# Holding back five of six early loads until VectorE's first memset has ended

## The chip, the cores and the metric

The kernel runs on one core of a Trainium2 chip. The metric is device time in microseconds (us) of one execution, as the median of several runs. One more execution was recorded by the hardware profiler; all views of the profile below are of that one.

## The reference

Scores of an attention layer, without the softmax: for each of 8 x 8 pairs of batch and head, every one of 512 queries with every one of 512 keys.

```
q, k: (8, 8, 512, 64) float32
scale = 1 / sqrt(64)
out[b, h, i, j] = sum over d of q[b, h, i, d] * k[b, h, j, d] * scale     # (8, 8, 512, 512) float32
```

The inputs are 16.8 MB, the output is 67.1 MB.

## The kernel before

The batch is worked through in four units of two batches each (`UNITS = 4`). A unit has one tile of k and one of q, each 128 partitions x 16 KB, so there are eight loads of 2 MB; they are numbered here load 0 (k of unit 0), load 1 (q of unit 0), load 2 (k of unit 1) and so on to load 7. Each unit gives four chunks of output (`CHUNKS = 4`), and each of the 16 chunks is stored with one DMA of 4 MB. Three large buffers (`bigs`) serve both the loaded tiles and the finished chunks.

The way of the data: SyncE issues a load (`load`, L78). GpSimd waits for it to land, and casts it to bf16 in two halves, in an order that suits the next step (L122, into `xb`); after the second half it raises `ready`. TensorE transposes the casts through an identity matrix (L130), moving two bf16 values as one float32 word. ScalarE and VectorE copy the transposes to `kT` and `qz` (L184). `qz` holds each query block beside zeros, and the zeros are written once, at the start, by two memsets on VectorE (L189), each raising `zeroed` by one. Then TensorE multiplies (L145), eight pairs of matmuls for a chunk, and ScalarE (L209) and VectorE (L212) take turns in scaling the pairs into the chunk's buffer. When both have done four, SyncE issues the store (L96).

The order on each engine is the order in which the program lists its instructions; semaphores, written out by hand, hold the engines together. The only part inside the scheduler's frame is load 0: `tc.close()` at L84 ends the frame, and its barriers stand at L85 in the profile. So load 0 is issued ahead of the barriers, and all else follows them.

On SyncE everything goes through one queue, in this order: load 0; the barriers; loads 1 to 5, with no wait between them; load 6 after `ready` has reached 3, and load 7 after it has reached 4, since these two fill a buffer again that an earlier unit used; then the 16 stores, each behind its waits for ScalarE and VectorE; and at the end the waits for the last stores.

VectorE's list begins, behind the barriers, with the two memsets of `qz`, and then goes on to the copies of the first transposes. GpSimd's begins with the identity matrix and then waits for load 0. On ScalarE the third copy waits until `zeroed` is 2, as does VectorE's.

Of the kernel before, what the change touches and what calls it, by code (L numbers as in the profile page):

```python
# [5 lines left out]
def kernel(  # L6
# [5 lines left out]
    nc = tc.nc  # L12
# [25 lines left out]
    sem = {name: nc.alloc_semaphore(name) for name in names}  # L38
# [38 lines left out]
    def load(v, x):  # L77
        nc.sync.dma_start(out=xf(v)[:, x],  # L78
                          in_=(k_r, q_r)[x][v].rearrange("p (s c) -> p s c", s=2)
                          ).then_inc(load_sems[2 * v + x], 16)  # L80
# [4 lines left out]
    tc.compile()  # L85


    for n in range(1, 2 * (UNITS - 1)):
        load(n // 2, n % 2)
    for x in range(2):  # L90
# [154 lines left out]
```

## Time and profile before

| | us |
|---|---|
| median of 3 runs | 201.34 (201.3 to 201.4) |
| the profiled execution | 201.4 |
| its span, from the first to the last instruction | 200.1 |
| load 0, issue to landing | 7.84 |
| load 1, issue to landing | 11.3 |
| a store, issue to landing, median | 21.9 |
| a cast of half a load on GpSimd (16 of them) | 2.46 |
| a memset of `qz` on VectorE (2) | 3.47 |

Times in the views are counted from the start of the span. SPq is SyncE's queue: its rows are the instructions that issue DMAs, and their duration is the time that SyncE spends on issuing, not that of the transfer. The transfer shows as "issue to landing", or as "DMA" in the chain of waits. A "window" is a stretch of the span: the view gives the busy time of each engine in it, the granted clock of TensorE, the busy share of the 16 DMA engines and the rate in GB/s. DMA engines are not to be confused with the engines that compute; a load of 128 rows of 16 KB is 128 packets, eight for each DMA engine, and a packet is counted in the window in which it starts.

### The profile page before, as it was taken

The page shows a single profiled execution, that of the slowest core. Times are in us where ns is not written, and L with a number is a line of the kernel's source. Part 1 is how long each engine was busy: PE and PEld are TensorE (multiplying, and loading weights), DVE is VectorE, ACT ScalarE, POOL GpSimd, SP SyncE. Part 2 cuts the span into 40 slices and gives each one's busy share as a digit, 9 for nine tenths or more (in the row PEclk, how much of TensorE's full clock was granted, in tenths as well). Part 3 has the DMA queues.
Part 4 walks back from the last instruction along what each step waited for, and adds up shares of the span by engine and source line. Part 5 has one row for each costly group of instructions (what it writes and reads, how often), then busy time and mean ns, then how long its engine had stood idle before and what let it go on. Part 6 is the DMA issues. An engine that isn't in the chain of part 4 may idle for free.

```text
span 200.1 us, 1081 instructions
## 1 busy us (share of the span) xinstructions
PE 100.4 (50%) x377; PEld 47.6 (24%) x384; DVE 106.1 (53%) x98; ACT 84.7 (42%) x97; POOL 39.4 (20%) x22
## 2 busy tenths in 40 slices
PE   0027660376785966376547646872737373830000
PEld 0026530142431532143124313330202020200000
DVE  3825692076796679276917682767364544450000
ACT  2004670264694657265626653664444443430000
POOL 1299999996000000000000000000000000000000
PEclk9999997579797599889957995799696968585555
DMA  6999999999999999999999999999999999999996
GB/s 197 426 423 436 439 429 423 426 409 429 416 442 436 429 423 436 436 426 429 429 432 436 429 426 439 429 429 423 439 426 432 423 442 429 429 426 429 432 439 259
DMA packets 5509, 83.95 MB, mean 420 GB/s; under 512 B 384, under 2 KB 384, under 8 KB 384
## 3 DMA queue, kind: packets, MB, share of 16 engines
q1 hardware_dynamic: 5504, 83.89, 98.6%
q8 instruction: 3, 0.05, 0.1%
q14 instruction: 2, 0.02, 0.0%
HBM read 16.78 MB, written 67.11 MB: 419 GB/s over the span
## 4 chain that ended last, share of the span: by engine, by line
DMA 54%; DVE 12%; POOL 12%; PE 10%; issue 1%; SPq 0%
DMA out_dram<-big 42%; POOL xb L122 12%; DVE big L212 10%; DMA big<-in_q_dram 7%; PE ps L145 7%; DMA big<-in_k_dram 4%; PE tp L130 3%; DVE qz L184 2%; DVE kT L184 1%; SPq L95 0%; SPq L85 0%; SPq L82 0%
## 5 line engine op out<-in xcount | busy, mean ns | idle before, releaser
L145 PE MATMUL ps<-kT,qz 128*128 128x512 bf16 x249 | 80.0, 455 | 61.3 <-DMA out_dram<-big 31.5
L212 DVE TENSOR_SCALAR big<-ps 128x1024 f32<-128x1024 f32 x64 | 77.0, 1223 | 52.0 <-PE ps L145 50.0
L209 ACT ACTIVATE big<-ps 128x1024 f32<-128x1024 f32 x64 | 65.0, 1023 | 70.8 <-PE ps L145 67.8
L145 PEld LDWEIGHTS ps<-kT,qz 128*128 128x128 bf16 x256 | 25.3, 110 | 109.4 <-DMA out_dram<-big 34.9
L122 POOL CAST xb<-big 128x2048 bf16<-128x2048 f32 x16 | 38.7, 2463 | 6.4 <-DMA big<-in_k_dram 5.8
L130 PE MATMUL tp<-identity,xb 128*128 128x128 f32 x104 | 19.6, 352 | 13.8 <-POOL xb L122 13.8
L130 PEld LDWEIGHTS tp<-identity,xb 128*128 128x128 f32 x104 | 17.6, 188 | 17.6 <-issue 16.3
L184 DVE COPY kT<-tp 64x512 f32<-64x512 f32 x14 | 9.7, 694 | 9.2 <-PE tp L130 8.8
L184 ACT COPY kT<-tp 64x512 f32<-64x512 f32 x14 | 8.1, 577 | 14.4 <-PE tp L130 14.2
L184 DVE COPY qz<-tp 64x512 f32<-64x512 f32 x12 | 8.3, 694 | 4.4 <-PE tp L130 4.0
L189 DVE MEMSET qz<- 128x4096 uint32 x2 | 6.9, 3472 | 4.1 <-PEq L85 3.3
L184 ACT COPY qz<-tp 64x512 f32<-64x512 f32 x12 | 7.4, 620 | 2.1 <-PE tp L130 2.0
L130 PE MATMUL ps<-identity,xb 128*128 128x128 f32 x24 | 5.4, 414 | 1.2 <-POOL xb L122 1.2
L130 PEld LDWEIGHTS ps<-identity,xb 128*128 128x128 f32 x24 | 5.0, 227 | 1.6 <-POOL xb L122 1.6
L184 DVE COPY qz<-ps 64x512 f32<-64x512 f32 x4 | 2.8, 694 | 1.9 <-PE ps L130 1.7
L184 ACT COPY qz<-ps 64x512 f32<-64x512 f32 x4 | 2.5, 632 | 2.2 <-PE ps L130 2.2
L184 ACT ACT_TABLE_LOAD x1 | 1.3, 1283 | 2.3 <-PEq L85 2.3
L184 DVE COPY kT<-ps 64x512 f32<-64x512 f32 x2 | 1.4, 694 | 0.3 <-PE ps L130 0.3
L184 ACT COPY kT<-ps 64x512 f32<-64x512 f32 x2 | 1.2, 578 | 0.5 <-PE ps L130 0.5
L102 POOL MEMSET identity<- 128x128 f32 x1 | 0.2, 204 | 1.9 <-POOLq L85 1.9
L104 POOL TENSOR_SCALAR_AFFINE_SELECT identity<-identity 128x128 f32<-128x128 f32 x1 | 0.3, 292 | 0.2 <-POOL identity L102 0.2
L229 POOL MEMSET const-float32-0.0<- 128x1 f32 x1 | 0.1, 98 | 0.2 <-issue 0.2
(3 smaller groups left out, 0.3 us busy)
## 6 DMA issues: line engine op xcount, KB each, us to landing
out_dram<-big SPq DMA_DIRECT2D x16, 4096.0 KB, 21.9
big<-in_k_dram SPq DMA_DIRECT2D x4, 2048.0 KB, 15.2
big<-in_q_dram SPq DMA_DIRECT2D x4, 2048.0 KB, 17.5
```

The source lines that it names most:

```text
L102: nc.gpsimd.memset(identity, 0.0).then_inc(sem["ident"], 1)
L104: nc.gpsimd.affine_select(out=identity, in_=identity, compare_op=mybir.AluOpType.not_equal, fill=1.0, base=0, pattern=[[-1, P]], channel_m ...
L122: cast = nc.gpsimd.tensor_copy(out=dst, in_=src)
L130: ins = pe.transpose(out=dst[:, w], identity=identity, in_=xw[:, c % SLOTS * W + w])
L145: ins = pe.matmul(out=pss[pair % 3][:, w, :], lhsT=qz[:, n, i + w], rhs=keys[:, n], start=True, stop=True)
L184: copy(out=dst, in_=src[:, h]).then_inc(sem["moved"], 1)
L189: engine.memset(qz[:, v * N:(v + 1) * N], 0.0).then_inc(sem["zeroed"], 1)
L209: lambda o, ps: nc.scalar.mul(out=o, in_=ps, mul=scale),
L212: lambda o, ps: nc.vector.tensor_scalar(out=o, in0=ps, scalar1=scale, scalar2=None, op0=mult),
L229: nc = _bacc.Bacc("TRN2", target_bir_lowering=False, num_devices=1)
```

## The change

SyncE gets one more wait, behind the barriers and ahead of load 1: it goes on once `zeroed` is at least 1, that is, once VectorE's first memset of `qz` has ended. Load 0 stays where it is. Loads 1 to 5, and all that SyncE issues behind them, stand behind the new wait. No other engine's list changes.

```diff
     tc.compile()
 
 
+    nc.sync.wait_ge(sem["zeroed"], 1)
     for n in range(1, 2 * (UNITS - 1)):
         load(n // 2, n % 2)
     for x in range(2):
         nc.sync.wait_ge(sem["ready"], 3 + x)
         load(UNITS - 1, x)
```

Line numbers behind the new line are one higher in the changed kernel: L78 stays L78, the cast at L122 becomes L123.

## The prediction

> **What bounds the kernel now.** I read the page first, then the chain of waits in order of time, then the start of the timeline, the DMA answer and the windows cut into the first 8.45 us. The page says at once who is busy:
>
> ```profile
> PE 100.4 (50%) x377; PEld 47.6 (24%) x384; DVE 106.1 (53%) x98; ACT 84.7 (42%) x97; POOL 39.4 (20%) x22
> ...
> DMA  6999999999999999999999999999999999999996
> ...
> DMA 54%; DVE 12%; POOL 12%; PE 10%; issue 1%; SPq 0%
> ```
>
> No engine passes 53%, while the DMA row stands at 9 in every slice but the first and the last. The chain names POOL, PE and DVE too, but during all of these steps the DMA engines go on moving queued bytes. So the time is the time of 84 MB through 16 DMA engines plus whatever they idle; from 8.45 us on they idle nowhere. Any idle that the change opens at the start is therefore paid at the end, unless something levels it out. The place to look is the start:
>
> ```profile
> 0.95 0.39 SPq L78 DMA_DIRECT2D big<-in_k_dram  x1
> 2.34 0.34 SPq L78 DMA_DIRECT2D big<-in_q_dram  x1
> ...
> 3.27 3.47 DVE L189 MEMSET qz<- 128x4096 uint32 x1 [3.27 <-PEq L85]
> ...
> 4.28 0.50 SPq L78 DMA_DIRECT2D big<-in_q_dram  x1
> 7.54 3.47 DVE L189 MEMSET qz<- 128x4096 uint32 x1 [0.80 <-issue]
> ...
> 0.95 7.84 DMA big<-in_k_dram
> 8.79 0.05 issue
> 8.85 4.81 POOL xb L122 x2
> 13.66 0.05 issue
> 13.71 4.84 POOL xb L122 x2
> ```
>
> Load 0 is issued at 0.95 and lands at 8.79. Loads 1 to 5 are issued from 2.34 to 4.78. VectorE's first memset runs from 3.27 to 6.74. The last lines are the chain of waits. Load 1's own row gives 11.3 us from issue to landing, so it lands at 2.34 + 11.3 = 13.64, and the second pair of casts starts behind it at 13.71: GpSimd works in step with the arriving loads, with hardly any slack.
>
> The windows tell how the DMA engines start (last two columns: mean busy share of the 16 engines, by the packets that start in the window, and GB/s):
>
> ```profile
> 0.95:1.95 1.00, 0.00 (x0) 0.00 (x0) 0.00 (x0) 0.00 (x0) 0.00 (x0) 1.00 0.00 0
> 1.95:2.40 0.45, 0.00 (x0) 0.00 (x0) 0.00 (x0) 0.06 (x1) 0.06 (x1) 1.00 2.61 473
> 2.40:4.30 1.90, 0.00 (x0) 0.00 (x0) 1.03 (x1) 1.23 (x1) 0.44 (x2) 1.00 0.66 241
> 4.30:7.65 3.35, 0.00 (x0) 0.00 (x0) 2.55 (x2) 0.00 (x0) 0.00 (x0) 1.00 0.98 416
> 7.65:8.45 0.80, 0.00 (x0) 0.00 (x0) 0.80 (x1) 0.00 (x0) 0.00 (x0) 1.00 1.01 430
> 8.45:42.00 33.55, 15.98 (x70) 11.42 (x72) 15.53 (x16) 11.91 (x16) 32.84 (x14) 0.85 1.01 428
> ```
>
> Nothing moves for 1.0 us after load 0's issue. Then 13 of the 16 engines begin within 0.45 us (473 GB/s x 0.45 us = 13 packets of 16 KB), each with a packet of 2.61 x 0.45 x 16 / 13 = 1.45 us. In the full stream 16 KB at 430 GB/s over 16 engines take 0.61 us, so a first packet costs 0.84 us extra. From 7.65 on the rate is full and stays so. The DMA answer for that stretch shows the hand-over from load 0 to load 1:
>
> ```profile
> DMA packets 23, 0.20 MB, mean 492 GB/s; under 512 B 11, under 2 KB 11, under 8 KB 11
> ...
> DMA packets 14, 0.15 MB, mean 328 GB/s; under 512 B 5, under 2 KB 5, under 8 KB 5
> ```
>
> The first line is 7.6 to 8.0, the second 8.0 to 8.45. The packets under 512 B are the completion writes, one for each engine: 11 engines finish load 0 in the first stretch, 5 in the second, none before 7.6. They take up load 1 at once, since the windows show no dip. So the engines come free between 7.65 and 8.45, on the mean near 7.95.
>
> **The change part by part.** Nothing is removed; one wait is added on SyncE, ahead of load 1. Queued behind it on SyncE are loads 1 to 5, the two loads with waits of their own, and all 16 stores. *Release:* the memset ends at 6.74, and the chain's hand-over from VectorE to a SyncE issue (63.13 to 63.19) is 0.06, so load 1 is issued near 6.80 in place of 2.34, 4.46 later. The other four follow it as now, over 2.44 us, the last ending at 9.24. Load 2 is wanted by the first engine only some 4.9 us after load 1 begins (8 packets x 0.61), near 12.7, so loads 2 to 5 cost nothing. Loads 6 and 7 are issued now at 23.48 and 28.41 while five queued loads keep the engines busy to about 33; the first store is issued at 31.12 with loads 6 and 7 still ahead of it until about 43. These covers are 8 us and more, and both issue and queue move by the same shift.
>
> *What 4.46 us of delay become:* load 1 now lies in the queue until the engines finish load 0, at 7.65 to 8.45, so most of the delay is waiting that vanishes. What is left is a hand-over with the queue nearly empty, and the trace has exactly one start of that kind, load 0's. Low end: load 1's first packets start 1.0 us after its issue, at 7.80, and run at the full rate at once; the first engines idle 0.15 us, the late ones not at all: about +0.1. High end: load 1 starts as load 0 did. With 7.84 us from issue to landing it lands at 6.80 + 7.84 = 14.64 in place of 13.65: +1.0. By engines it is the same: 13 begin 1.0 to 1.45 after the issue and 3 by about 2.0 (2.40 to 3.00 shows 82 GB/s, three packets), on the mean some 1.25; 6.80 + 1.25 = 8.05 against 7.95, and 0.84 for the slow first packet, +0.94.
>
> A rule of the Trainium skill bears on this. The row is the empty 1.0 us after the issue at 0.95, and the 1.45 us of the first packets behind it. "DMA: Bandwidth & Descriptors", section "Latency and other measured facts", gives about 600 ns to the first byte for a DMA from this queue; by that, an estimate from the page, load 1's bytes would be there at 7.40, before any engine is free, and the sum would be +0, or 201.4. The trace's row is longer, and it is used. The same page's section "Rules for kernel authors" speaks against the change: issue the DMA early and wait late, since the fixed setup cost then overlaps; in the trace of before it does overlap, with no dip at 7.65.
>
> I take +0.75, near the high end: load 0's start is the nearest row (same queue, instruction and size). I leave out a quarter of it because load 0 starts in the middle of the barriers, with the issues of five other loads from 2.34 on, and because the engines are still at work when load 1's descriptors come.
>
> *After that:* the casts of load 1 wait for a landing 0.75 later, GpSimd idles that long, and the loads and stores behind move alike. Nothing makes it up, because the DMA engines had no idle time to give back. The memsets themselves stay as they are: both last 3472 ns, whatever load is landing. The profiled execution took 201.4 us with a span of 200.1, 1.3 outside it; 201.4 + 0.75 = 202.15, and the median of the three runs is 0.06 lower: 202.1.
>
> **The rivals.** *The wait hides (201.5).* The engines are busy until 7.65, load 1 is issued 0.85 before that, and its first packet, being fetched beside running transfers, costs 0.61 as all later ones do. Then the sum is its low end, +0.1, at most +0.4. For it: the slow first packets appear only at the cold start; load 1's at 7.65 to 8.45 were not slow, though they were the first from q. Against it: those came from a full queue.
>
> *Faster (200.9).* Between 2.40 and 4.30 the rate is 241 GB/s where 430 is usual, which loses 1.90 x (1 - 241/430) = 0.84 us, just while SyncE issues five more loads (0.43 to 0.52 us for four of them, against 0.33 for the same instruction at 23.48). If these issues slow load 0, moving them away lets it finish up to 0.84 earlier, at 6.8 to 7.6. Load 1 can't begin before 7.80, so the early engines lose 0.15 at least; but the engine that is late, free at 8.45 now, could begin between 7.80 and 8.05 and gain 0.4 to 0.6. The span ends with the last engine, so the whole would gain about 0.45. It decides if the late engine of load 0 is also the last one at the end, and if load 1's own start isn't slow, two conditions. Against it: loads 2 to 5 would now be issued in the middle of load 1's start, 0.34 us behind it.
>
> *More than the start (203.1).* The same disturbance, now on load 1: 0.84 us on top of the 1.0, +1.8. Or the release comes not at the memset's end but 0.8 later, where the second memset begins (7.54), with +0.75 on top of the 1.0. Against the latter: other VectorE results reach SyncE in 0.06.
>
> That the wait doesn't hold at all is no rival: the order of SyncE's instructions shows it on load 1, and the memset takes its 3.47 us in any case.
>
> **How the numbers follow.** A queue that starts slowly again, from +0.4 to +1.25: 0.62, own range 201.75 to 202.6. The wait hides, from 0 to +0.4: 0.26. Faster: 0.06. More than the start: 0.06. Two runs of this kernel can be told apart from about 0.2%, or 0.4 us. So slower by more than that is 0.62 + 0.06 = 0.68, same 0.26, faster 0.06. The range that holds 8 in 10 must take in the likeliest case and most of the hidden one: 201.3 to 202.6.
>
> **What would show it.** Right: load 1's issue at 6.8 in the timeline, its row of issue to landing falling from 11.3 to between 7.2 and 7.9, a dip of the GB/s somewhere from 7.6 to 10, POOL idle 0.4 to 1.0 us ahead of the cast at L123, all later landings moved by the same amount, and the DMA row at 9 to the end. Wrong: no dip behind 7.65 and load 1 landing at 13.7 (the wait hides); load 0 landing well before 8.79 and the last completion earlier (faster); load 1 issued near 7.6 or landing after 15 (more); or a landing that moves while the end doesn't, in which case the sixteen engines' unequal finish, not their sum, sets the time.

## The result, and the profile after

| | before | changed |
|---|---|---|
| median of 4 runs, us | 201.36 | 202.45 |
| lowest to highest | 201.3 to 201.4 | 202.25 to 202.5 |
| span of the profiled execution | 200.1 | 201.2 |

The changed kernel is 1.09 us slower: ratio 1.0053, 95% interval 1.0035 to 1.007.

The chain of waits of the changed kernel now begins with the memset and SyncE (start, duration, what):

```profile
3.27 3.48 DVE qz L190
...
6.77 0.34 SPq L78
```

Load 1 is issued at 6.77; its row of issue to landing says 7.8 us where it said 11.3, and GpSimd is late for its casts. The start of the timeline:

```profile
6.77 0.34 SPq L78 DMA_DIRECT2D big<-in_q_dram  x1
...
8.75 4.81 POOL L123 CAST xb<-big 128x2048 bf16<-128x2048 f32 x2 [5.68 <-DMA big<-in_k_dram]
...
14.63 7.36 POOL L123 CAST xb<-big 128x2048 bf16<-128x2048 f32 x3 [1.08 <-DMA big<-in_q_dram]
```

The casts of load 1 begin at 14.63 in place of 13.71, 0.92 later. (GpSimd idles 1.08 us ahead of them, 0.10 of it because load 0 landed 0.10 sooner and its casts ended sooner.) The windows of the changed kernel show what the DMA engines do (last two columns: mean share of the 16 engines, GB/s):

```profile
2.40:4.30 1.90, 0.00 (x0) 0.00 (x0) 1.03 (x1) 1.23 (x1) 0.44 (x2) 1.00 0.62 233
...
7.65:8.45 0.80, 0.00 (x0) 0.00 (x0) 0.80 (x1) 0.00 (x0) 0.00 (x0) 1.00 1.73 369
8.45:9.50 1.05, 0.00 (x0) 0.00 (x0) 1.05 (x1) 0.00 (x0) 0.75 (x1) 1.00 0.66 203
9.50:42.00 32.50, 14.92 (x65) 10.42 (x67) 14.48 (x16) 11.43 (x16) 31.16 (x14) 0.86 1.01 428
42.00:197.50 155.50, 83.34 (x314) 36.33 (x318) 86.22 (x81) 72.00 (x81) 6.81 (x3) 0.81 1.00 429
```

Between 7.65 and 8.45, where before the share was 1.01 at 430 GB/s, it is now 1.73 at 369. 369 GB/s for 0.80 us are 18 packets of 16 KB, 1.73 x 0.80 x 16 = 22.1 us of engine time: 1.2 us for a packet, in place of 0.61. So most engines do not stand empty; they begin load 1's first packet in time and take twice as long for it. Added up from the trace's packet records, the packets of 16 KB that start between 7.3 and 12 us took 0.88 us for each engine more than 0.61 apiece would make; before, they took nothing more. The 203 GB/s that follow are the echo: a packet is counted where it starts, and few can start while so many drag on. From 9.50 to 42 the rate is on the mean that of before, and the loss is never made up.

The trace's completion records show the shift engine by engine. Load 1 was complete on the mean engine at 13.22 and on the last at 13.65; now these are 14.06 and 14.58. The last completion of the kernel moves from 200.06 to 201.16. Of the 1.1 us, 0.93 is there when load 1 has landed; the other 0.2 appears while load 7 lands (44.40 in place of 43.28). Several of the experiments lose more at that place; it is taken up at their end.

### The profile page after: what moved, and what is told of

Its sections match the earlier page's. It is cut to its first block, busy times and chain, and to the rows that moved or that the text cites. A ratio compares the mean times of both kernels' runs of the same rounds, so it can differ in the third digit from the quotient of the medians.

```text
span 201.2 us, 1081 instructions
## 1 busy us (share of the span) xinstructions
PE 98.3 (49%) x377; PEld 46.8 (23%) x384; DVE 106.1 (53%) x98; ACT 84.7 (42%) x97; POOL 39.4 (20%) x22
## 4 chain that ended last, share of the span: by engine, by line
DMA 56%; DVE 14%; PE 9%; POOL 7%; issue 1%; ACT 1%; SPq 0%
DMA out_dram<-big 42%; DVE big L213 9%; DMA big<-in_q_dram 7%; POOL xb L123 7%; DMA big<-in_k_dram 6%; PE ps L146 6%; PE tp L131 3%; DVE qz L185 2%; DVE qz L190 2%; DVE kT L185 1%; ACT big L210 1%; SPq L78 0%; SPq L96 0%
## 5 line engine op out<-in xcount | busy, mean ns | idle before, releaser
L146 PE MATMUL ps<-kT,qz 128*128 128x512 bf16 x249 | 78.1, 443 | 63.0 <-DMA out_dram<-big 32.2
L146 PEld LDWEIGHTS ps<-kT,qz 128*128 128x128 bf16 x256 | 24.6, 109 | 109.7 <-DMA out_dram<-big 35.4
L123 POOL CAST xb<-big 128x2048 bf16<-128x2048 f32 x16 | 38.7, 2464 | 7.5 <-DMA big<-in_k_dram 5.7
```

The lines of the kernel that those rows point to most:

```text
L123: cast = nc.gpsimd.tensor_copy(out=dst, in_=src)
L146: ins = pe.matmul(out=pss[pair % 3][:, w, :], lhsT=qz[:, n, i + w], rhs=keys[:, n], start=True, stop=True)
```

## The experiments

All times are medians, each beside runs of the kernel before on the same chip (201.4 to 201.5). "Mean" and "last" are the completions of load 1 over the 16 DMA engines, from the trace of one profiled execution, which need not be the median one: that of e3 was its slowest, 203.89.

**How early is early enough (e1, e10, e2, e3).** The first memset is made shorter and the second longer, so that the wait lets go earlier:

```diff
-            for v in range(2):
-                engine.memset(qz[:, v * N:(v + 1) * N], 0.0).then_inc(sem["zeroed"], 1)
+            for lo, hi in ((0, 4), (4, 2 * N)):
+                engine.memset(qz[:, lo:hi], 0.0).then_inc(sem["zeroed"], 1)
```

This is e1. In e10 the 4 is 5, in e2 it is 6, in e3 it is 7.

> The first memset clears 4 of 16 blocks of qz, the second the other 12, so the wait lets go near 3.27 + 1.74 = 5.0 and load 1 is issued near 5.07. Theory 'start time' (a load issued into a queue that runs dry takes 7.8 us to land, so the shift is the larger of 0 and issue + 7.8 - 13.65): load 1 lands at 13.65, as before; 201.4. Rival 'step' (a second start costs its 1.0 us whenever it comes): load 1 lands near 14.6; 202.4. Rival 'crowding' (loads 2 to 5, issued right behind load 1, slow its first packets): load 1 lands between 13.65 and 14.6, as its first packets are slow here too.

> As before, with 6 of 16 blocks in the first memset: release near 5.87, load 1 issued near 5.94. 'Start time': 5.94 + 7.8 = 13.74, +0.1; 201.45. 'Step': load 1 near 14.6; 202.4.

> With 7 of 16 blocks in the first memset: release near 6.31, load 1 issued near 6.37. 'Start time': 6.37 + 7.8 = 14.17, +0.5; 201.9. 'Step': near 14.6; 202.4.

e10 was added after these three:

> 5 of 16 blocks in the first memset: the release falls between e1's (4.6, no cost) and e2's (5.67, +1.0), so load 1 is issued near 5.16, 2.5 us before the first engine is free. A cost that grows with the delay: +0.0 to +0.3, 201.4 to 201.7. A step: either 201.4 or 202.4 and nothing between.

| | load 1 issued | mean | last | time | ratio to before |
|---|---|---|---|---|---|
| before | 2.34 | 13.22 | 13.65 | 201.4 | 1 |
| e1 | 4.62 | 13.19 | 13.62 | 201.47 | 1.0 (0.9991 to 1.0008) |
| e10 | 5.17 | 13.79 | 14.51 | 202.16 | 1.0027 (1.0018 to 1.0037) |
| e2 | 5.70 | 13.63 | 15.26 | 202.52 | 1.0047 (1.0034 to 1.006) |
| e3 | 6.22 | 13.56 | 14.60 | 202.57 | 1.0067 (1.0043 to 1.0091) |
| changed | 6.77 | 14.06 | 14.58 | 202.45 | 1.0053 (1.0035 to 1.007) |

The law "issue plus 7.8" held for e1 and for the changed kernel and failed between: e2 was to pay 0.1 by it and paid 1.0. A plain step failed too, since the median of e10 lies between; its ten runs spread from 201.53 to 202.54, from no price to the full one, where those of before on that chip spread by 0.5 us. What is shown is that load 1 costs nothing if issued about 3 us before the engines come free (from 7.65 on), and most of the full price at 2 us. The windows of e1 and then of e2:

```profile
7.65:8.45 0.80, 0.00 (x0) 0.00 (x0) 0.80 (x1) 0.00 (x0) 0.00 (x0) 1.00 1.11 471
8.45:9.50 1.05, 0.00 (x0) 0.00 (x0) 1.05 (x1) 0.00 (x0) 0.68 (x1) 1.00 0.91 390
```

```profile
7.65:8.45 0.80, 0.00 (x0) 0.00 (x0) 0.80 (x1) 0.00 (x0) 0.00 (x0) 1.00 1.23 389
8.45:9.50 1.05, 0.00 (x0) 0.00 (x0) 1.05 (x1) 0.00 (x0) 0.65 (x1) 1.00 0.78 312
```

e1's rate swings around 430, e2's dips, but by less than the changed kernel's: the mean engine loses only 0.4 there. Its last engine loses 1.6. The DMA answer of e2 for three stretches of 1 us from 12.3 on counts the completions of load 1, which are the packets under 512 B:

```profile
DMA packets 35, 0.43 MB, mean 426 GB/s; under 512 B 9, under 2 KB 9, under 8 KB 9
...
DMA packets 32, 0.43 MB, mean 426 GB/s; under 512 B 6, under 2 KB 6, under 8 KB 6
...
DMA packets 27, 0.43 MB, mean 426 GB/s; under 512 B 1, under 2 KB 1, under 8 KB 1
```

Nine, six, and one straggler; before and in the changed kernel all 16 fell into one of these stretches. A load has landed when its last engine has. The end of the kernel can't be told from load 1's last engine alone, though: in e2 that is 1.6 late and the end of the span 1.1, in e3's profile 0.95 and 2.46.

**A long delay (e4).**

```diff
-    nc.sync.wait_ge(sem["zeroed"], 1)
+    nc.sync.wait_ge(sem["zeroed"], 2)
```

> The wait is for both memsets (zeroed at 2), which end at 11.02: load 1 issued near 11.05. 'Start time': it lands at 11.05 + 7.8 = 18.85, 5.2 later than before, and the kernel takes 206.6, since nothing gives the time back. 'Step' with its fixed 1.0 on top of the engines' idle time (7.95 to 12.05, 4.1): 5.1, hardly to be told apart; if later stages have slack, less than that: 203 to 206.

206.7 us, 1.026 (1.0247 to 1.0273), with load 1 issued at 11.03 and landing at 18.59. Into a queue that is empty the landing takes 7.6 to 7.8 us, as it does for load 0, and the delay goes through to the end undiminished: +5.3 on the median, +4.94 at load 1's landing. No later stage has slack.

**Which load pays (e5).**

```diff
+    load(0, 1)
     nc.sync.wait_ge(sem["zeroed"], 1)
-    for n in range(1, 2 * (UNITS - 1)):
+    for n in range(2, 2 * (UNITS - 1)):
         load(n // 2, n % 2)
```

> The wait stands behind load 1 in place of ahead of it: load 1 is issued at 2.34 as before, loads 2 to 5 from 6.8 on. 'Start time': load 1 lands at 13.65; load 2 needs 6.8 + 7.8 = 14.6 at the latest and lands in the queue's turn at 18.5; 201.4, so the whole cost of the change is load 1's. Rival 'total hold' (any of the five held back costs): 201.6 to 202.4.

201.39, ratio 0.9994 (0.9986 to 1.0003): no difference. Loads 2 to 5 are issued from 6.76 on, within 0.4 us of the changed kernel's (from 7.16 on), and cost nothing. Without load 1's delay there is no price.

**Crowding (e6, e8, e9).** Loads 2 to 5 are held until load 0 has landed, so that nothing is issued while load 1 starts. e6 is the changed kernel with this, e8 is e2 with it, e9 is e3.

```diff
     nc.sync.wait_ge(sem["zeroed"], 1)
-    for n in range(1, 2 * (UNITS - 1)):
+    load(0, 1)
+    nc.sync.wait_ge(load_sems[0], 16)
+    for n in range(2, 2 * (UNITS - 1)):
         load(n // 2, n % 2)
```

> As the changed kernel, but loads 2 to 5 wait until load 0 has landed (8.7), so that SyncE issues nothing while load 1 starts. 'Start time': as changed, load 1 lands at 14.6; 202.4. 'Crowding': the first packets of load 1 lose their extra 0.84, load 1 lands at 13.75 to 14.0; 201.5 to 201.8.

202.51, 1.0046 (1.0031 to 1.0061), mean 14.05, last 14.32. The window after the hand-over of e6 is as slow as in the changed kernel:

```profile
7.65:8.45 0.80, 0.00 (x0) 0.00 (x0) 0.80 (x1) 0.00 (x0) 0.00 (x0) 1.00 1.81 369
8.45:9.50 1.05, 0.00 (x0) 0.00 (x0) 1.05 (x1) 0.00 (x0) 0.69 (x1) 1.00 0.43 140
```

So the slow first packets are load 1's own, not the work of the loads behind it.

> As e2 (load 1 issued near 5.70), but loads 2 to 5 wait until load 0 has landed, so nothing is issued behind load 1 until 8.8. In e2 the mean completion of load 1 over the 16 DMA engines came 0.4 later than before, but the last engine 1.6 later (15.26). Theory 'stragglers by crowding' (where a few engines run dry, the issues of loads 2 to 5 hold up the descriptors of load 1 on some): the last completion of load 1 falls to about 13.7 to 14.0 and the time to 201.4 to 201.8. Rival 'slow start alone' (the engines are slow for some 3 us after any issue into a short queue): stragglers stay, last completion 14.5 or later, 202.3 to 202.5.

> As e3 (load 1 issued near 6.22), with loads 2 to 5 held until load 0 has landed. 'Stragglers by crowding': last completion of load 1 near 6.22 + 7.8 = 14.0, time near 201.8. 'Slow start alone': last completion 14.6, time 202.3 to 202.6.

e8: 202.93, 1.0069 (1.0057 to 1.0081), last 15.44. e9: 202.96, 1.007 (1.0053 to 1.0086), last 15.74. The theory that crowding makes the stragglers falls: with nothing behind load 1 they stay, and neither kernel is faster than e2 or e3. By the medians both are slower by 0.4, but the intervals of the ratios overlap, and for e9 and e3 the ratios are alike (1.007 and 1.0067).

**Smaller packets (e7).** The changed kernel, with load 1 as two loads of half the columns; GpSimd waits for both.

```diff
+    for s in range(2):
+        nc.sync.dma_start(out=xf(0)[:, 1, s],
+                          in_=q_r[0].rearrange("p (s c) -> p s c", s=2)[:, s]
+                          ).then_inc(load_sems[1], 16)
```

> As the changed kernel, but load 1 is two loads of half the columns, so its packets are 8 KB. If a first packet has a fixed extra of 0.84 us whatever its size: load 1 lands near 14.6, 202.4. If it is slow in proportion (2.4 times its 0.31 us): 0.7 us are saved, load 1 lands near 13.9, 201.75.

202.75, 1.0063 (1.0046 to 1.0079). Neither expectation is met: the second half is complete on the mean engine at 13.91 and on the last at 14.22, some 0.15 and 0.36 sooner than in the changed kernel, and yet the time is no better; what was saved here was lost again near load 7 (below). Inconclusive on the size of the extra, and no way to save it.

**The same price elsewhere (e11).** Load 1 is issued early, as in e5, but loads 2 to 5 wait for both memsets, so that now load 2 comes late to engines that have been streaming for 9 us:

```diff
+    load(0, 1)
+    nc.sync.wait_ge(sem["zeroed"], 2)
-    for n in range(1, 2 * (UNITS - 1)):
+    for n in range(2, 2 * (UNITS - 1)):
         load(n // 2, n % 2)
```

> As e5 (load 1 issued at 2.34), but loads 2 to 5 wait for both memsets, so load 2 is issued near 11.03, some 1.4 us before the first engine has finished load 1 (12.5). If the price is that of any hand-over with less than some 3 us between the issue and the engines' coming free (e1 had 3.1 and paid nothing): load 2 lands 0.4 to 1.0 later on the mean than its 18.1 of before, with slow packets near 12.5 to 14; 201.9 to 202.6. If it belongs to the second DMA of the kernel, or to the first microseconds (cold memory, the barriers): load 2 lands at 18.1 to 18.5, no slow packets; 201.4.

203.66, 1.0117 (1.0097 to 1.0136). Load 2 is issued at 11.04, and the first engines finish load 1 at 12.2. One window of e11, and the same of before:

```profile
12.40:13.40 1.00, 0.00 (x0) 0.00 (x0) 0.00 (x0) 0.00 (x0) 1.00 (x1) 1.00 0.58 180
```

```profile
12.40:13.40 1.00, 0.00 (x0) 0.00 (x0) 0.00 (x0) 0.00 (x0) 1.00 (x1) 1.00 0.89 377
```

Load 2 is complete on the mean engine 0.9 later than before (19.00 in place of 18.11) and on the last 2.25 later (20.80 in place of 18.55). The mean is within the 0.4 to 1.0 expected. So the price is one of a late hand-over, and not of the kernel's first microseconds. The time moves by 2.2, more than expected; this looks like the last engine's 2.25, but over 16 engines the mean of the last store's completions is 1.95 later than before, and that of load 2's only 0.9. Some 1.0 us is lost further on.

**A second loss, near load 7 (all profiles).** Up to load 6 the lateness of the mean engine stays as it was at the hand-over; at load 7, the last load, it grows. In us against before, at load 6 and then at load 7: changed kernel 0.84 and 1.05, e4 5.08 and 5.18, e6 0.83 and 0.90, e2 0.43 and 0.86, e3 0.36 and 1.04, e7 0.69 and 1.31, e8 0.29 and 1.29, e9 0.42 and 0.76, e11 0.93 and 1.86. In e1 and e5, which pay nothing, both are within 0.05 of before, and in e10 it doesn't grow (0.58 and 0.46). The windows from 40 to 45 us of before, the changed kernel, e2 and e11:

```profile
40.00:45.00 5.00, 3.63 (x17) 2.31 (x16) 3.60 (x5) 3.20 (x4) 4.72 (x3) 0.77 1.02 413
40.00:45.00 5.00, 4.37 (x18) 2.60 (x16) 3.05 (x4) 3.62 (x5) 4.53 (x3) 0.71 0.98 380
40.00:45.00 5.00, 4.69 (x19) 2.54 (x17) 2.73 (x4) 3.57 (x5) 4.64 (x2) 0.71 1.01 367
40.00:45.00 5.00, 4.59 (x18) 2.80 (x19) 1.92 (x3) 2.75 (x4) 4.92 (x3) 0.61 0.97 315
```

The engines are nearly as busy as before and move less: packets are slow here too. Those of 16 KB that start between 40 and 50 us take 0.30 us for each engine more than 0.61 apiece in the kernel before, 0.48 in the changed kernel, 0.75 in e2 and 1.20 in e11. So the price of e2, e3, e7, e8, e9 and e11 has two parts, one at the hand-over and one here. What makes packets slow here was not tested. Engines out of step with each other are not a full answer: those of e7 are within 0.7 us at load 6, and it loses 0.6.

## Why the prediction was right, and where it was off

*The bound.* Right. The DMA engines lost time and gave none of it back; e4 shows the same for five times the loss.

*Release and queue.* Right: load 1 issued at 6.77 against 6.80, and the four loads behind it free, which e5 shows by itself.

*Load 1's start.* The high end was the right row. A landing at 14.64 was worked out from load 0's start, and 14.58 was measured. The term that was mis-sized is the quarter taken off: +0.75 at load 1's landing, where +0.93 came. Of its reasons, the disturbance of load 0's start by five issues is refuted by the changed kernel's own windows: with no issue of any load between 0.95 and 6.77, the stretch 2.40 to 4.30 still runs at 233 GB/s, against 241 before. The barriers stand in both kernels; in e4 load 1, far from them, took 7.56 us to land, against 7.64 to 7.85 for load 0 in the thirteen profiles, so they are worth 0.1 to 0.3 at most.

*After that.* Nearly right. The loads and stores behind were to move alike, and up to load 6 they did; the other 0.2 of the 1.09 came at load 7, a term the prediction had at nothing.

*What the engines do meanwhile.* Right for the high end, wrong for the low one. The prediction counted 0.1 us of idle engines and 0.84 of slow packet; the slow packets of the trace add up to 0.88 for each engine, and little is left for idling. But the low end's condition, that load 1 runs at the full rate if the engines are still busy 1.0 us after its issue, was far too kind. By e1, e10 and e2 it takes some 3 us of lead before the hand-over is free.

*The wait hides.* Fell. A lead of 0.85 us was thought possibly enough; even 2 us (e2) were not.

*Faster.* Fell. It needed load 0 to land up to 0.84 earlier without the other issues; it landed at 8.69 in place of 8.79, within the 8.59 to 8.80 of all the profiles.

*More than the start.* Fell for this change: e6 takes the suspected disturbance away and gains nothing. The release came at the memset's end.

*The rules.* By the estimate from the Trainium skill's first-byte figure ("DMA: Bandwidth & Descriptors", "Latency and other measured facts", about 600 ns) the change was free. In these traces the first packet of a load into an empty queue starts 1.0 us after its issue begins (1.96 against 0.95; in e4 12.0 against 11.03), which is 0.6 after the issuing instruction has ended (1.34; in e4 11.37); counted from there the figure agrees. What costs the time is that the data come slowly for a while after that. The same page's advice to issue early is what e1 and e5 bear out, and these runs put a number to early: about 3 us.

*Left open.* What makes the first packets slow, and why with a lead of 1.2 to 2 us (e2, e3, e8, e9, e11) one or two DMA engines end up 0.6 to 1.8 us behind the others, was not settled. It isn't the loads behind (e6, e8, e9), nor the start of the kernel (e11). The second loss, near load 7, is open too.

## What to carry to other kernels

Where DMA engines are the bound, keep the next transfer in their queue well before they finish the last one; here 3 us of lead were free and 2 us cost 1 us for good. A transfer further back in the queue may be issued late without harm as long as it keeps such a lead (load 2 in e5, not in e11), so a wait belongs behind the one that the engines will take next. And follow a hand-over to the end of the kernel: in e2 the mean engine was only 0.4 late behind it, and the end moved by 1.1.

## What the runs showed of the hardware that was not expected

The record of a memset on VectorE does not hold all of the time that a longer one takes. e1's two memsets, and then the changed kernel's:

```profile
2.83 1.76 DVE L190 MEMSET qz<- 128x2048 uint32 x1 [2.83 <-PEq L85]
5.82 5.18 DVE L190 MEMSET qz<- 128x6144 uint32 x1 [1.23 <-issue]
```

```profile
3.27 3.47 DVE L190 MEMSET qz<- 128x4096 uint32 x1 [3.27 <-PEq L85]
7.54 3.47 DVE L190 MEMSET qz<- 128x4096 uint32 x1 [0.80 <-issue]
```

Both kernels leave the barriers alike, but the longer memset starts 0.44 later in the record, and the gap ahead of the second grows with the second's length (0.80 for 4096 elements, 1.23 for 6144). For 2048 elements more in each partition, start and duration together grow by 0.44 + 1.71 = 2.15 us, 0.95 elements per ns, so about a fifth of what a longer memset takes stands as idle time ahead of it. That is why load 1 came at 4.62 in e1 and not at the 5.07 expected. The Trainium skill gives VectorE 0.96 GHz ("Trainium Kernel Development and Optimization", "NeuronCore Architecture"), which fits one element a cycle for the sum, not for the recorded duration alone.

Some DMA engines seem to stand idle in a late hand-over while others go on: in e11's window above, packets for only 0.58 of the engines' time begin, though load 2 had been issued 1.4 us before the window opens. In the changed kernel's, 7.65 to 8.45, they began in time and were slow. By the packet records of e11, slow packets between 12 and 20 us make up 0.49 of the 0.89 us by which load 2's mean completion is late, so some 0.4 is engines without a packet. Which form comes when is open.
